# One-hot rows and weighted copies of the expert routing for eight tokens at once on VectorE, in 16-bit pairs

## The chip, the core and the metric

The kernel runs on one NeuronCore of a Trainium2 chip. Its engines are TensorE (PE in the profile, PEld for its weight loads), VectorE (DVE), ScalarE (ACT), GpSimd (POOL) and SyncE (SP, which issues most of the DMAs). Each engine works through its own queue in order and waits on semaphores for the others. The metric is the device time of one execution in microseconds; lower is better.

## What is computed

A 256-token model of two blocks, batch 1, width 1024, float32. The first block has three mixers side by side (state space, gated recurrence, retention) and a convolutional feed-forward network (FFN below). The second block has two layers over two streams of 256 tokens, latents and context; each layer mixes tokens (convolution, mLSTM, differential attention) and then applies PEER, a feed-forward layer of 16,384 small experts. The change concerns PEER:

```python
def peer_ffn(h, wq, sub_keys, eu, ev):
    def one(t):                                   # 128 tokens
        q = (t @ wq).reshape(128, 8, 2, 64)
        s = einsum("thpd,hpnd->thpn", q, sub_keys)
        st, it = top_k(s, 16)                     # of 128 keys, two halves
        cand = st[:, :, 0, :, None] + st[:, :, 1, None, :]
        cidx = it[:, :, 0, :, None] * 128 + it[:, :, 1, None, :]
        best, pos = top_k(cand, 16)
        e = take_along_axis(cidx, pos)            # 8 heads x 16 experts a token
        g = softmax(best)
        act = gelu(einsum("thkd,td->thk", eu[e], t))
        return einsum("thk,thkd->td", g * act, ev[e])
```

## The kernel before

PEER is computed densely. For every expert e = 128 n1 + n2 the products of all tokens with `eu` are formed, the gelu of them is multiplied by a dense matrix A[e, token] that holds the sum of the weights g of an expert chosen by that token and zero elsewhere, and the result goes through `ev`. Weights arrive as 512 KB pieces (`raw`); each is split into a high part on ACT (`whi`, L254) and a low part on DVE or POOL by turns (`wlo`, L255), and a product is 24 matmuls: high by high, high by low and low by high, over 8 k-tiles (L296, L297, L299).

A is made by `spread` (L1363 to L1400) from `sl`, which `choose` leaves for 128 tokens at a time: the two key numbers i1, i2 of each of the 128 slots (8 heads x 16), and g in two float16 parts. Slots lie on partitions. For each token a one-hot row over n1 and one over n2 is made by comparing an iota with i1 and i2; the row of n1 is multiplied by the two parts of g; two matmuls of 128x128 contract over the slots and add the token's A[n1, n2]. This goes in pieces of 4 tokens: two comparisons on DVE (`o2` L1375, `o1` L1380, 128x512, float32 in and float16 out), the weighted copies `ow` by shares on POOL (L1384), DVE (L1390) and ACT (L1392), 8 matmuls (L1395) into one of two PSUM banks, a copy into `stg` on ACT (L1396). Four pieces fill `stg` (1 MB), which SP writes to DRAM (L1399). 32 pieces make one call of `spread`; there are six calls.

In layer 0 `peer` runs both streams (512 columns a matmul). Its first 64 tiles of the first product (`first`, 24 matmuls and a gelu into `gt`, L1462) run "ahead", and the routing's pieces are recorded between them: half a tile for each piece of `choose`, then `early` (the context stream's two calls of `spread`, 100 pieces a tile for the first and 3 for the second), then the latents' two calls, 3 pieces a tile. In layer 1 (256 columns a matmul, 104 tiles ahead) 1.3 pieces of `spread` go with a tile. A scheduler then sets the order of each engine's queue from the dependences, a cost model and the recorded order, so the first call of `early` has filled gaps of the token mixing that stands before `peer`.

SBUF tiles lie in pools on a left and a right stack. A pool that takes the address range of an earlier one waits until that one is released. One such place matters below: the FFN of the first block (`ff8`: its normed input `fh`, `fl` and its hidden tiles) is on the left, while the context stream's token mixing of layer 0 runs on the right; the lowest of its pools is `m01d`, of the differential attention. In the program before, `ff8` ends at byte 128,608 of a partition and `m01d` begins at byte 128,704.

## Time and profile before

| | us |
|---|---|
| median of 3 runs (lowest to highest) | 4106.46 (4102.27 to 4113.05) |
| profiled execution, first to last instruction | 4098.2 |
| PE busy | 3722.7 (91%) |
| DVE busy | 2698.6 (66%) |
| ACT busy | 1785.9 (44%) |
| POOL busy | 1406.0 (34%) |

Shares of the whole span are averages over stages with different limits. The six calls of `spread` fall into three stretches: 986 to 1300 us (the first call of `early`, in gaps of the latents' token mixing), 1455 to 1770 us (the second call and the latents' two, in layer 0's ahead stage) and 3345 to 3592 us (layer 1). A stretch is read by four things: how busy each engine is in it, at what granted clock TensorE ran (1.00 is 2.4 GHz, 0.5 is 1.2 GHz, values between are mixtures), what TensorE waited for, and how many pieces and tiles were done.

### The profile page before, as it was taken

How to read it: one execution, taken by the hardware profiler on the slowest of the kernel's cores; microseconds unless marked ns; L12 is line 12 of the kernel's file. 1: busy time of each engine (PE TensorE's matmuls, PEld its weight loads, DVE VectorE, ACT ScalarE, POOL GpSimd, SP SyncE). 2: the span in 40 equal slices, each digit the busy share in tenths (PEclk: the TensorE clock that was granted, in tenths of full speed). 3: DMA queues.
4: the chain of work that ended last, by engine and by line, in shares of the span. 5: the costliest groups of instructions: out<-in, count | busy, mean ns of one | idle time of the engine just before them, and what ended most of it. 6: DMA issues, size and time to landing. Idle time of an engine off the chain costs nothing. (4 is left out here: it accounts for less than half of the span.)

```text
span 4098.2 us, 62119 instructions
## 1 busy us (share of the span) xinstructions
PE 3722.7 (91%) x23599; PEld 3237.8 (79%) x23599; DVE 2698.6 (66%) x5543; ACT 1785.9 (44%) x2944; POOL 1406.0 (34%) x904
## 2 busy tenths in 40 slices
PE   7899987987879988799999999999988887899998
PEld 6599987986857766677788888888876887789898
DVE  6745668689687788945553344443764899976765
ACT  3444456444565354432322233332462446644443
POOL 1132314255445675631111111111242557732222
PEclk9999998998989998999999999999999999999999
DMA  6654532443325444475663333433425546696764
GB/s 236 220 171 157 165 127 70 139 144 124 119 95 181 144 167 168 152 236 175 192 188 118 113 119 118 126 106 98 142 96 177 162 147 206 208 287 193 237 217 141
DMA packets 284122, 653.71 MB, mean 160 GB/s; under 512 B 21296, under 2 KB 139824, under 8 KB 277552
## 3 DMA queue, kind: packets, MB, share of 16 engines
q1 hardware_dynamic: 282960, 647.24, 48.7%
q8 instruction: 185, 3.03, 0.3%
q10 hardware_dynamic: 720, 1.47, 0.1%
q14 instruction: 113, 0.93, 0.1%
q0 software_dynamic: 144, 1.05, 0.1%
HBM read 574.70 MB, written 74.97 MB: 159 GB/s over the span
## 5 line engine op out<-in xcount | busy, mean ns | idle before, releaser
L255 POOL TENSOR_TENSOR wlo<-raw,whi 128x1024 fp32r<-128x1024 f32 x360 | 893.9, 2484 | 1994.4 <-ACT whi L254 836.5
L254 ACT ACTIVATE whi<-raw 128x1024 fp32r<-128x1024 f32 x836 | 882.4, 1057 | 1371.9 <-PE pp L1545 521.8
L255 DVE TENSOR_TENSOR wlo<-raw,whi 128x1024 fp32r<-128x1024 f32 x476 | 612.2, 1286 | 334.1 <-ACT whi L254 258.0
L296 PE MATMUL pp<-Hh,whi 128*128 128x256 f32 (+1 forms) x2176 | 717.5, 349 | 4.3 <-ACT whi L254 3.1
L297 PE MATMUL pp<-Hl,whi 128*128 128x256 f32 (+1 forms) x2176 | 705.9, 344 | 0.0
L1544 PE MATMUL pp<-yh,whi 128*128 128x512 f32 (+1 forms) x2048 | 650.6, 340 | 18.0 <-ACT yh L254 16.3
L1545 PE MATMUL pp<-yl,whi 128*128 128x512 f32 (+1 forms) x2048 | 654.1, 341 | 12.6 <-DVE yl L255 12.5
L296 PEld LDWEIGHTS pp<-Hh,whi 128*128 128x128 f32 x2176 | 427.1, 197 | 50.6 <-ACT whi L254 3.9
L297 PEld LDWEIGHTS pp<-Hl,whi 128*128 128x128 f32 x2176 | 427.3, 197 | 44.3 <-DVE ow L1390 0.9
L1544 PEld LDWEIGHTS pp<-yh,whi 128*128 128x128 f32 x2048 | 386.5, 190 | 67.8 <-ACT yh L254 23.7
L299 PE MATMUL pp<-Hh,wlo 128*128 128x256 f32 (+1 forms) x2176 | 420.0, 336 | 21.4 <-DVE wlo L255 19.4
L1545 PEld LDWEIGHTS pp<-yl,whi 128*128 128x128 f32 x2048 | 388.4, 191 | 62.1 <-DVE yl L255 19.2
L1549 DVE SCALAR_TENSOR_TENSOR xT<-pp,mod,xT 128x256 f32<-128x256 f32 x256 | 123.0, 481 | 443.0 <-PE pp L1547 442.6
L1547 PE MATMUL pp<-yh,wlo 128*128 128x512 f32 (+1 forms) x2048 | 398.2, 337 | 0.3 <-POOL wlo L255 0.3
L299 PEld LDWEIGHTS pp<-Hh,wlo 128*128 128x128 f32 x2176 | 343.0, 191 | 65.5 <-DVE wlo L255 21.0
L1547 PEld LDWEIGHTS pp<-yh,wlo 128*128 128x128 f32 x2048 | 323.9, 189 | 42.5 <-POOL wlo L255 0.5
L1531 DVE TENSOR_TENSOR gt<-gt,At 128x512 f32<-128x512 f32 (+1 forms) x256 | 206.2, 821 | 116.7 <-ACT gt L1462 70.2
L1395 PE MATMUL pm<-o,ow 128*128 128x128 f16 x1536 | 131.2, 229 | 121.9 <-DVE ow L1390 87.6
L1384 POOL TENSOR_TENSOR ow<-o,sl 128x512 f16<-128x512 f16 x128 | 187.8, 1472 | 135.2 <-DVE o L1380 115.7
L1395 PEld LDWEIGHTS <-ow 128*128 128x128 f16 x1536 | 97.6, 101 | 165.7 <-DVE ow L1390 124.0
L254 ACT ACTIVATE yh<-gt 128x512 fp32r<-128x512 f32 (+1 forms) x256 | 124.5, 518 | 225.3 <-DVE gt L1531 225.0
L1396 ACT ACTIVATE stg<-pm 128x512 f32<-128x512 f32 x192 | 192.7, 1056 | 61.7 <-PE pm L1395 41.4
(457 smaller groups left out, 6691.0 us busy)
## 6 DMA issues: line engine op xcount, KB each, us to landing
raw<-pu SPq DMA_DIRECT2D x256, 512.0 KB, 3.8
raw<-pv SPq DMA_DIRECT2D x256, 512.0 KB, 3.8
raw<-w SPq DMA_DIRECT2D x136, 512.0 KB, 3.6
aw<-ada SPq DMA_DIRECT2D x96, 512.0 KB, 4.4
A<-stg SPq DMA_DIRECT2D x48, 1024.0 KB, 5.7
At<-A SPq DMA_DIRECT2D x48, 1024.0 KB, 7.9
raw<-wf SPq DMA_DIRECT2D x72, 512.0 KB, 3.6
raw<-wo SPq DMA_DIRECT2D x32, 512.0 KB, 4.2
```

The costliest lines, as they stand in the source:

```text
L254: A.activation(hi, src, AF.Copy)
L255: (eng or V).tensor_sub(lo, src, hi.bitcast(F32))
L296: PE.matmul(ps, wh[:, k], xh[:, x0 + k], start=start and j == 0, stop=False)
L297: PE.matmul(ps, wh[:, k], xl[:, x0 + k], start=False, stop=False)
L299: PE.matmul(ps, wl[:, k], xh[:, x0 + k], start=False, stop=stop and j == len(ks) - 1)
L1384: G.tensor_mul(ow[:, na:], o1[:, na:, None].to_broadcast([P, nw, 2, P]), sl[:, 2:4, t0 + na:t0 + 4].rearrange("p j e -> p e j")[:, :, :, None]
L1395: PE.matmul(ps[:, e * P:(e + 1) * P], ow[:, e, j], o2[:, e], start=j == 0, stop=j == 1)
L1396: A.activation(stg[:, :, 4 * q4:4 * q4 + 4].rearrange("p n e -> p e n"), ps.rearrange("p (e n) -> p e n", e=4), AF.Copy, scale=1.0 / GSCALE)
L1531: V.tensor_mul(gt.rearrange("p (a t) -> p a t", t=16), gt.rearrange("p (a t) -> p a t", t=16), At[g][:, :, j])
L1544: PE.matmul(ps, wh[:, j], yh, start=j == 0, stop=False)
L1545: PE.matmul(ps, wh[:, j], yl, start=False, stop=False)
L1547: PE.matmul(ps, wl[:, j], Y[g, j][0], start=False, stop=j == 7)
```

## The change

`spread` handles 8 tokens (TB) at a time. The tile `sl` becomes float16 and holds every number twice: i1 beside i2, each as [token][n1 or n2], then g's high part beside its low part, with pairs that have the layout [2 kinds][token][pair]. An iota in float16, `iota16` (256 bytes a partition, in the permanent pool `perm`), is made once. One comparison on DVE gives the one-hot rows of both n1 and n2 of 8 tokens (`oo`, 128x2048, all operands float16, innermost dimension of two neighbouring elements) and one product on DVE gives both weighted copies (`ow`, 128x2048). POOL and ACT make none any more. The matmuls are the same in number and size; a piece is now every second token of a block, so that `stg` holds [n2 group][4 token pairs][8 n2][2 tokens] and the copy from PSUM writes elements 8 bytes apart where it wrote them 64 bytes apart. A keeps its size in DRAM; the multiplication in the main stage reads it in runs of 2 elements where it read runs of 16. `oo` and `ow` have two buffers each, in `early` `ow` has one. Layer 1 keeps 51 tiles in SBUF where it kept 52.

```diff
+    iota16 = perm.tile([P, P], F16, name="iota16")
+    V.tensor_copy(iota16, iota)
...
-        A.activation(sl[:, :2].rearrange("p j t -> p (j t)"), pt[:, :2 * P], AF.Copy)
-        hi = sm.tile([P, P], F16, name="ghi")
-        A.activation(hi, pt[:, 2 * P:3 * P], AF.Copy, scale=GSCALE)
-        V.tensor_copy(sl[:, 2], hi)
-        V.scalar_tensor_tensor(sl[:, 3], pt[:, 2 * P:3 * P], GSCALE, hi, op0=ALU.mult, op1=ALU.subtract)
+        twice = [P, P, 2]
+        for j in range(2):
+            A.activation(sl[:, 0, :, j], pt[:, j * P:(j + 1) * P][:, :, None].to_broadcast(twice), AF.Copy)
+        g = pt[:, 2 * P:3 * P][:, :, None].to_broadcast(twice)
+        A.activation(sl[:, 1, :, 0], g, AF.Copy, scale=GSCALE)
+        V.scalar_tensor_tensor(sl[:, 1, :, 1], g, GSCALE, sl[:, 1, :, 0], op0=ALU.mult, op1=ALU.subtract)
...
-    def spread(sl, Ad, t, sm, bank, share):
+    def spread(sl, Ad, t, sm, bank, ows=2):
+        wide = [P, TB, 2, P // 2, 2]
         for tg in range(8):
-            stg = sm.tile([P, P, 16], F32, name="stg")     # [n1][n2][16 t]
-            for q4 in range(4):
...
-                o2 = sm.tile([P, 4, P], F16, name="o2", bufs=O2)
-                if nd:
-                    V.tensor_tensor(o2[:, :nd], iota[:, None].to_broadcast([P, nd, P]),
-                                    sl[:, 1, t0:t0 + nd][:, :, None].to_broadcast([P, nd, P]), op=ALU.is_equal)
...
-                V.tensor_tensor(o1, iota[:, None].to_broadcast([P, 4, P]),
-                                sl[:, 0, t0:t0 + 4][:, :, None].to_broadcast([P, 4, P]), op=ALU.is_equal)
...
-                    G.tensor_mul(ow[:, na:], o1[:, na:, None].to_broadcast([P, nw, 2, P]),
...
-                            V.tensor_scalar(ow[:, e, j], o1[:, e], sl[:, 2 + j, t0 + e:t0 + e + 1], None, op0=ALU.mult)
...
-                        A.activation(ow[:, e, j], o1[:, e], AF.Copy, scale=sl[:, 2 + j, t0 + e:t0 + e + 1])
...
+            stg = sm.tile([P, 16, 8, 8, 2], F32, name="stg")
+            for b in range(16 // TB):
+                t0 = tg * 16 + b * TB
+                ix, gg = [sl[:, m, t0:t0 + TB][:, :, :, None].to_broadcast(wide) for m in range(2)]
+                oo = sm.tile([P, TB, 2, P], F16, name="oo", bufs=2)
+                V.tensor_tensor(oo.rearrange("p t j (n k) -> p t j n k", k=2),
+                                iota16.rearrange("p (n k) -> p n k", k=2)[:, None, None].to_broadcast(wide), ix,
+                                op=ALU.is_equal)
+                ow = sm.tile([P, TB, 2, P], F16, name="ow", bufs=ows)
+                V.tensor_tensor(ow.rearrange("p t j (n k) -> p t j n k", k=2),
+                                oo[:, :, 0].rearrange("p t (n k) -> p t n k", k=2)[:, :, None].to_broadcast(wide), gg,
+                                op=ALU.mult)
+                for k in range(2):
+                    ps = bank()
+                    for e in range(4):
+                        for j in range(2):
+                            PE.matmul(ps[:, e * P:(e + 1) * P], ow[:, 2 * e + k, j], oo[:, 2 * e + k, 1],
+                                      start=j == 0, stop=j == 1)
+                    A.activation(stg[:, :, 4 * b:4 * b + 4, :, k].rearrange("p g e n -> p e g n"),
+                                 ps.rearrange("p (e g n) -> p e g n", e=4, g=16), AF.Copy, scale=1.0 / GSCALE)
...
-            V.tensor_mul(gt.rearrange("p (a t) -> p a t", t=16), gt.rearrange("p (a t) -> p a t", t=16),
-                         At[g][:, :, j])
+            gv = gt.rearrange("p (a e k) -> p a e k", e=8, k=2)
+            V.tensor_mul(gv, gv, At[g][:, :, :, j])
...
-        peer(1, (0,), 13, 4, 52)
+        peer(1, (0,), 13, 4, 51)
```

The 256 bytes of `iota16` move every pool of the left stack up by as much. In the program after, `ff8` ends at byte 128,864, which is 160 bytes above the start of `m01d`.

DVE's queue in the latents' `spread` of layer 0 (`sl`; line 1375 is the comparison in both programs, 1380 the second one of before, 1390 the products of before, 1379 the product of after). Before:

```order
L1375 TENSOR_TENSOR o2_17427<-gen_65,sl_13240 128x512
L1380 TENSOR_TENSOR o1_17429<-gen_65,sl_13240 128x512
L1380 TENSOR_TENSOR o1_17483<-gen_65,sl_13240 128x512
L1390 TENSOR_SCALAR ow_17431<-o1_17429,sl_13240 128x128 x4
L1380 TENSOR_TENSOR o1_17505<-gen_65,sl_13241 128x512
L1375 TENSOR_TENSOR o2_17481<-gen_65,sl_13240 128x512
L1390 TENSOR_SCALAR ow_17485<-o1_17483,sl_13240 128x128 x4
```

And after:

```order
L1375 TENSOR_TENSOR oo_16504<-iota16_71,sl_13240 128x2048
L1379 TENSOR_TENSOR ow_16506<-oo_16504,sl_13240 128x2048
L1375 TENSOR_TENSOR oo_16530<-iota16_71,sl_13240 128x2048
L1379 TENSOR_TENSOR ow_16532<-oo_16530,sl_13240 128x2048
L1375 TENSOR_TENSOR oo_16588<-iota16_71,sl_13240 128x2048
```

Six instructions of DVE for every 4 tokens have become two for every 8, and nothing else stands between them.

DVE's queue where the first call of `early` (`ksl`) runs among the final norm of the first block (`rq`, `xT`). Before:

```order
L1380 TENSOR_TENSOR o1_14905<-gen_65,ksl_5211 128x512
L330 SCALAR_TENSOR_TENSOR rq_10731<-rq_10731 128x2
L1375 TENSOR_TENSOR o2_14923<-gen_65,ksl_5211 128x512
L1390 TENSOR_SCALAR ow_14907<-o1_14905,ksl_5211 128x128
L782 SCALAR_TENSOR_TENSOR xT_60<-xT_60,par_67,pm_10698 128x256 x8
L1390 TENSOR_SCALAR ow_14907<-o1_14905,ksl_5211 128x128
```

And after:

```order
L1375 TENSOR_TENSOR oo_14918<-iota16_71,ksl_5213 128x2048
L329 SCALAR_TENSOR_TENSOR rq_10731<-rq_10731 128x2
L1379 TENSOR_TENSOR ow_14894<-oo_14892,ksl_5213 128x2048
L330 TENSOR_TENSOR rq_10731<-rq_10731 128x2
L331 SCALAR_TENSOR_TENSOR rq_10731<-rq_10731 128x2
L783 SCALAR_TENSOR_TENSOR xT_60<-xT_60,par_67,pm_10698 128x256 x8
L1379 TENSOR_TENSOR ow_14920<-oo_14918,ksl_5213 128x2048
```

The same gaps are taken, by instructions four to sixteen times as wide; the second `ow` here has to wait until TensorE has read the first, because there is one buffer.

ACT's queue where the normed input `fh` of the FFN is first written (`kdk` is a projection of the context's token mixing, `pairh` the output of its attention). Before:

```order
L1007 ACTIVATE kdk_5208<-pp_5415 128x256
L254 ACTIVATE whi_5450<-raw_5448 128x1024
L361 ACTIVATE fh_7512<-t1_7562 128x256
L254 ACTIVATE whi_5482<-raw_5480 128x1024
L1007 ACTIVATE kdk_5208<-pp_5447 128x256
L361 ACTIVATE fh_7512<-t1_7566 128x256
```

And after:

```order
L255 ACTIVATE pairh_6189<-t1_6488 128x256
L255 ACTIVATE whi_6889<-raw_6887 128x1024
L1136 ACTIVATE t1_6639<-t1_6639 128x128
L1149 ACTIVATE t2_6644<-pp_6615 128x260
L255 ACTIVATE pairh_6189<-t1_6590 128x256
L362 ACTIVATE fh_7514<-t1_7564 128x256
```

`fh` has moved from the context's first projections to behind the last output of its attention, `pairh`, some 160 instructions further down ACT's queue. On TensorE's queue, with the other matmuls counted, 397 matmuls of the FFN stood ahead of the 4200th other one before, and 161 after. Of the second call of `early`, 2 pieces stood ahead of the choice of the latents' experts on TensorE's queue and 10 do now; from the latents' `spread` on, that queue is the same in both programs apart from names, but for a few matmuls near its end.

## Rows read from the trace of the kernel before

**Rows 1.** The page's first line.

```profile
span 4098.2 us, 62119 instructions
```

**Rows 2.** Busy time by stretch: PE, PEld, DVE, ACT, POOL; granted clock, DMA share, GB/s.

```profile
1455.00:1770.00 315.00, 255.27 (x1517) 200.86 (x1516) 293.20 (x477) 155.93 (x217) 195.48 (x123) 0.91 0.46 163
3345.00:3592.00 247.00, 199.98 (x1773) 191.59 (x1772) 238.48 (x333) 162.93 (x296) 171.78 (x95) 0.94 0.61 200
986.00:1300.00 314.00, 253.07 (x1713) 212.91 (x1712) 243.05 (x573) 183.16 (x393) 142.14 (x115) 0.87 0.37 124
...
520.00:674.00 154.00, 134.83 (x918) 120.72 (x918) 112.54 (x290) 99.45 (x219) 48.67 (x51) 0.97 0.28 93
674.00:1000.00 326.00, 276.30 (x2070) 265.10 (x2071) 265.43 (x737) 133.88 (x213) 140.06 (x97) 0.93 0.42 141
...
440.00:480.00 40.00, 40.00 (x340) 39.81 (x340) 29.96 (x35) 19.26 (x29) 10.37 (x5) 1.00 0.55 178
2000.00:2500.00 500.00, 498.87 (x2177) 408.06 (x2176) 219.00 (x293) 151.76 (x185) 72.59 (x30) 1.00 0.46 142
3600.00:3650.00 50.00, 46.42 (x361) 44.28 (x360) 40.80 (x75) 22.12 (x37) 14.66 (x6) 0.97 0.94 290
3700.00:4098.00 398.00, 370.69 (x3034) 364.85 (x3032) 245.15 (x370) 169.89 (x249) 101.43 (x41) 0.98 0.62 198
```

**Rows 3.** DVE's instructions on the one-hot rows alone, by stretch (busy, count).

```profile
986.00:1300.00 314.00, 77.07 (x146) 0.87 0.37 124
1455.00:1770.00 315.00, 290.67 (x474) 0.91 0.46 163
3345.00:3592.00 247.00, 189.46 (x239) 0.94 0.61 200
```

**Rows 4.** What PE waited for, 1455 to 1770 us: total, times, longest.

```profile
PE pm L1395 <- DVE ow L1390: 35.7, 28, 2.1
PE pm L1395 <- ACT stg L1396: 24.0, 30, 3.9
```

**Rows 5.** What PE waited for, 3345 to 3592 us.

```profile
PE pm L1395 <- DVE ow L1390: 40.3, 22, 2.9
```

**Rows 6.** ACT's copies into `stg` by stretch: one for each piece.

```profile
1455.00:1770.00 315.00, 91.40 (x95) 0.91 0.46 163
3345.00:3592.00 247.00, 65.72 (x62) 0.94 0.61 200
```

**Rows 7.** ACT's gelu into `gt` by stretch: one for each tile.

```profile
1455.00:1770.00 315.00, 19.12 (x32) 0.91 0.46 163
3345.00:3592.00 247.00, 19.33 (x53) 0.94 0.61 200
```

**Rows 8.** DVE by line: ns min/median/max, first and last start, forms.

```profile
L1375 DVE TENSOR_TENSOR o<-gen,sl x128: 673/680/2909, 1383.0 to 3592.1; 128x512 f16<-128x512 f32 x128
...
L1390 DVE TENSOR_SCALAR ow<-o,sl x384: 228/244/2451, 1387.7 to 3595.1; 128x128 f16<-128x128 f16 x192
...
L255 DVE TENSOR_TENSOR wlo<-raw,whi x476: 1154/1219/3433, 14.5 to 4076.1; 128x1024 fp32r<-128x1024 f32 x159
...
L373 DVE TENSOR_SCALAR t<-t x6: 172/276/841, 34.8 to 2912.1; 36x256 f32<-36x256 f32 x4, 16x256 f32<-16x256 f32 x1, 128x8 f32<-128x8 f32 x1
...
L380 DVE SCALAR_TENSOR_TENSOR t<-t,t x36: 158/406/949, 41.1 to 2924.2; 36x256 f32<-36x256 f32 x24, 16x256 f32<-16x256 f32 x6, 128x8 f32<-128x8 f32 x6
```

**Rows 9.** ACT by form: busy, mean ns of one, idle before and its releasers.

```profile
L1396 ACT ACTIVATE stg<-pm 128x512 f32<-128x512 f32 x192 | 192.7, 1056 | 61.7 <-PE pm L1395 41.4 <-issue 20.2
...
L1462 ACT ACTIVATE gt<-pp 128x512 f32<-128x512 f32 x128 | 76.5, 597 | 86.4 <-PE pp L299 84.2 <-DMA GX<-gt 1.4 <-DMA raw<-pu 0.7
```

**Rows 10.** POOL's splits `wlo` alone, 1455 to 1770 us.

```profile
1455.00:1770.00 315.00, 80.40 (x33) 0.91 0.46 163
```

**Rows 11.** PE's matmuls on `fh`, then on `fl`, 520 to 674 us.

```profile
520.00:674.00 154.00, 24.29 (x104) 0.97 0.28 93
...
520.00:674.00 154.00, 14.99 (x56) 0.97 0.28 93
```

More of the change, by code (lines that the diff above doesn't have):

```diff
@@ L25 @@
 GSCALE = 32768.0
-E0 = (0, 2, 1)
-O1, O2, OW = 2, 3, 3
+TB = 8
 def _cols(v):
@@ L1469, in peer @@
             q = queries(l, W, bk, sp, [z[:, :, j * T:(j + 1) * T] for z in (Hh, Hl)])
-            sls = [sp.tile([P, 4, P], F32, name="sl") for t in range(2)]
+            sls = [sp.tile([P, 2, P, 2, 2], F16, name="sl") for t in range(2)]
             bo = bo or Banks(ls, f"po{l}", 0, 2)
@@ L1485, in pieces @@
                     mark(f"spread{l}{s}")
-                    for _ in spread(sls[t], Ads[j], t, so, bo.misc, lambda n: (0, 2, ns)):
+                    for _ in spread(sls[t], Ads[j], t, so, bo.misc):
                         yield (1.3, 3.0)[1 - l]
@@ L1622, in build @@
                 a.wout()
-            early = [(100 if t == 0 else 3, spread(sls[t], A01, t, so, ax.misc, lambda n, t=t: E0)) for t in range(2)]
+            early = [(100 if t == 0 else 3, spread(sls[t], A01, t, so, ax.misc, 1)) for t in range(2)]
             def side(st):
```

34 lines of the change are left out of this document (7 added, 27 removed).

## The prediction

> **What bounds the kernel now.** I first read the page's span, 4098.2 us [rows 1], then the busy times by stretch, because the change touches only the stretches in which the expert matrix A is spread. In two of them DVE is the limit. From 1455 to 1770 us (layer 0, 512 columns) it is busy 293.2 of 315.0 us; from 3345 to 3592 us (layer 1, 256 columns) 238.5 of 247.0 us. PE is busy 81% in both, at a granted clock of 0.91 and 0.94 [rows 2]. What fills DVE there is the work that is replaced: 290.7 and 189.5 us on one-hot rows and their copies [rows 3]. PE waits for those copies: 35.7 us in the first stretch, with another 24.0 us for ACT's copy of a PSUM bank [rows 4], and 40.3 us in the second [rows 5]. The reader should also see that DVE's busy time holds waiting: a copy takes 0.244 us in the median and 2.451 us at worst, a comparison 0.680 and 2.909 [rows 8]. The longest are as long as one of POOL's splits, 80.4 us for 33 or 2.44 us each [rows 10]. In layer 0's stretch the 95 pieces hold 190 comparisons and 31 x 2 + 64 x 4 = 318 copies, 207 us by their medians; the other 84 of the 290.7 are hindrance, under 195 us of POOL's work. In the first spreading stretch, 986 to 1300 us, nobody is the limit: DVE 243 of 314 us, PE 253 [rows 2], and spreading is 77 us of it [rows 3].
>
> **What TensorE needs if nothing holds it up.** A 512-column matmul costs 498.87/2177 = 0.229 us at full clock, a 256-column one 40.00/340 = 0.118 us [rows 2]; for one of 128 columns I take a quarter of the first, 0.057 us. Layer 0's stretch has 95 pieces [rows 6] and 32 tiles [rows 7]: 32 x 24 x 0.229 + 95 x 8 x 0.057 = 176 + 43 = 219 us, against 315 that it takes. Layer 1's has 62 pieces and 53 tiles: 53 x 24 x 0.118 + 62 x 8 x 0.057 = 150 + 28 = 178 us, against 247. (The 8 pieces that the second call of `early` now puts ahead of the choice are 4 us of PE in either place.)
>
> **The new DVE instructions.** Two of 2048 columns for 8 tokens, so one for each piece of 4. No 16-bit instruction with two tensor inputs stands in the trace. Upper bound: two float32 inputs cost 0.680 us at 512 columns and 1.219 at 1024 [rows 8], 0.539 more for 512, so 2.30 us at 2048. Lower bound: as for half the columns, 1.22 us. I take the lower one. The trace shows that this engine does two columns a step where a form allows it: 256 columns take 0.276 us in a one-input instruction and 0.406 in a two-input one, in the same float32 [rows 8]; the new operands are laid out as pairs of 16 bits. The Trainium skill, page VectorE: DVE Perf Modes, section The perf-mode tier table, gives a 16-bit two-input instruction of 2048 columns 1224 ns and a float32 one 2293; by it the sum stands as I make it, and no run here shows it yet. Collisions with POOL add to either: 84 us under 195 us of POOL's work make about 34 under the 80 that stay, for 95 instructions some 0.3 us each.
>
> *Layer 0's stretch.* DVE: 95 x 1.22 = 116 us, 144 with collisions, far below 219, so PE sets the pace. To its 219 us come the waits for a PSUM bank: two banks stay, and these were 24.0 us. ACT's copy takes 1.056 us where a contiguous one of the same size takes 0.597 [rows 9]; the new writes are 8 bytes apart and not 64, the cost lies between these two, and I take half of the wait, 12 us. In the 16 blocks of `early` `ow` has one buffer: the next product waits for TensorE, which waits for it, 1.22 us at most where no tile stands between, some 11 times, 13 us; I take 8. Sum 239, a gain of 76. Bounds: 95 with neither wait, 36 with both whole and the clock left at 0.91 (219/0.91 + 37 = 278). ACT loses its share of the copies and POOL 116 us of work; neither was the limit, so that is worth nothing by itself.
>
> *Layer 1's stretch.* DVE: 62 x 1.22 = 76 us and the 49 us that are not spreading (238.5 less 189.5), 125 in all; with collisions 144. PE's 178 us is the floor, but the transfers come near: 200 GB/s over 247 us would have to pass in 178 us, 278 GB/s, and the densest stretch shows 290 at a DMA share of 0.94 [rows 2]. I take 195 us, a gain of 52; bounds 69 (PE alone) and 25 (DVE unpacked with collisions, 62 x 2.58 + 49 = 209, and 13 of other waits).
>
> *The first call of early.* Its 32 pieces leave DVE 39 us of work where 77 stood. DVE is one of several engines waited for there, so I take a quarter of the 38, a gain of 10. Bounds: all 38, and a loss of 20: with one buffer of `ow`, DVE can stand in front of each of 16 products for 1.22 us, and the norms and attention queued behind it on DVE, then PE and ACT, wait too.
>
> *iota16.* Its cast is one short instruction. Its 256 bytes are not free: `ff8` now reaches 160 bytes into `m01d`, so `fh` is not written before the context's attention is over. Before, TensorE did 104 + 56 = 160 of the FFN's matmuls by 674 us [rows 11], 160 x 0.118 = 19 us; by the queues the lag grows to 397 - 161 = 236 matmuls, 28 us. All of it costs if PE was idle there otherwise, nothing if the context's mixing ends earlier by as much. PE was busy 135 of 154 us until 674 and then 276 of 326 with DVE at 265 [rows 2], so both in part: a loss of 12, bounds 0 and 28.
>
> *Main stages.* The multiplication by A reads runs of 8 bytes. If that cost 0.23 us more for 256 columns (half of 1.056 less 0.597), layer 1's 128 would be 29 us of DVE, in a stretch where it is idle 153 of 398 us [rows 2]: 0, at most a loss of 10. In layer 0 PE is busy 498.87 of 500 us and hides it. The one tile more through DRAM is 128 KB each way, under 1 us.
>
> Sum: +12 - 10 - 76 - 52 + 0 = -126 us. On the profiled execution's 4098.2 us that is 3972; the median of the runs, 4106.46, lies 8.3 us higher, and 3980 is my time.
>
> **The rivals.** *Unpacked*: the instructions take 2.30 us. DVE then needs 95 x 2.58 = 245 us in layer 0 and 209 in layer 1, 6 and 14 more than the sum has, and the first call gains nothing (10): 3980 + 30 = 4010. Against it: the two-columns row; for it: that row is of another form.
>
> *Unpacked and in turn with POOL*: DVE and POOL wait for each other's whole instruction, so their times add. Layer 0: 95 x 2.30 + 80 = 299 us, 60 more than the sum; layer 1: 62 x 2.30 + 49 + 27 splits x 2.44 = 258, no gain but a start 11 us later, taken as 247 to 258 and 57 more; the first call 10: about 4107, no change. Packed, adding gives 116 + 80 = 196 us, and nothing changes. Against it: today 207 us of unhindered DVE work and 195 of POOL's fit into 315 us, so 87 us at least ran together; for it, the 2.45 us stalls. The Trainium skill, page SBUF — State Buffer, section SBUF: two separate sides, says that a DVE instruction with two SBUF inputs and a GpSimd one that reads SBUF take a shared port pair in turn, for the whole instruction; the stalls agree with it, the 87 us do not.
>
> *Side effects*: the FFN's lag costs its 28 and the first call its loss of 20: 3980 + 16 + 30 = 4026. For it: DVE and PE are both dense from 674 to 1000 us. Against it: PE is busy 88% of the time before 674 us, so the context's mixing has time to win there.
>
> *Slower*: pairs are read at a penalty, as ACT pays for scattered elements. The price from the same row is 0.46 us for 512 columns, so 2.30 + 4 x 0.46 = 4.14 us. Layer 0: 95 x 4.14 = 393, 78 more than now; layer 1: 62 x 4.14 + 49 = 306, 59 more; the first call 32 x 4.14 - 77 = 55, half of it; the FFN 12: 4106 + 176 = 4280. It decides from a mean of 3.3 us an instruction on (315/95), and 3.2 in layer 1. Nothing in the trace speaks for it but that ACT row.
>
> **How the numbers follow.** Forecast 0.72 (3900 to 4035), unpacked 0.11, in turn with POOL 0.04, side effects 0.09, slower 0.04. The bounds of the terms add up to -202 and about 0 us; all at one end is unlikely. The range 3900 to 4060 leaves out the slower case, the one in turn with POOL, and the tails of the others, under 2 in 10. Faster by over 0.3% (what a measurement of this kernel can tell from no change): 0.72 + 0.11 + 0.09 less a little, 0.91. Within 0.3%: 0.05. Slower: 0.04.
>
> **What would show it.** Right: the instructions of 2048 columns at 1.2 to 1.5 us; a tile and its three pieces in layer 0 every 7.5 us, where it was 9.8; PE's waits for DVE under 15 us in both stretches; DVE below 60% there; a clock near 1.00; `fh` first written near 685 us instead of 530. Wrong: instructions above 2 us; PE waiting for ACT or for transfers as long as it did for DVE; the context's mixing or the first call longer than before; a main stage that grows.

## The result, and the profile after

The changed kernel takes 3958.53 us (median of 4 runs, 3951.11 to 3968.15), the kernel before 4104.36 us beside it: a ratio of 0.9646 [0.9626, 0.9665], or 146 us less. The prediction was 3980, with a range of 3900 to 4060. The profiled execution of after has a span of 3966.4 us, 131.8 less than that of before [rows 1]; it is the longest of the four (3968.15 us), and the kernel's repetition below has a span of 3951.4.

The two stretches of spreading, busy times by stretch (columns: length; PE, PEld, DVE, ACT, POOL busy; granted clock; DMA share; GB/s). First layer 0 with 512 columns, then layer 1 with 256:

```profile
core 0: us, PE busy (x) PEld busy (x) DVE busy (x) ACT busy (x) POOL busy (x), PEclk, DMA share, GB/s
1478.00:1690.00 212.00, 202.62 (x1363) 162.99 (x1361) 139.47 (x79) 93.49 (x143) 69.33 (x30) 1.00 0.62 215
3285.00:3453.00 168.00, 166.88 (x1649) 164.71 (x1648) 136.60 (x86) 103.49 (x165) 66.72 (x24) 1.00 0.84 283
```

Where DVE was busy 93 and 97% and PE 81% [rows 2], PE is now busy 96 and 99% at full clock. What PE still waits for in the first of them (us in total, times, longest), where [rows 4] had 35.7 and 24.0:

```profile
PE pm L1387 <- DVE ow L1379: 7.8, 5, 1.8
PE pm L1387 <- ACT stg L1389: 1.4, 1, 1.4
```

In the second there is only one wait of 1.1 us, for `stg`, where [rows 5] had 40.3 us for `ow`.

The new instructions, by tile (shortest/median/longest in ns); `ksl` is the context's call, `sl` the latents' and layer 1's:

```profile
L1375 DVE TENSOR_TENSOR oo<-iota,ksl x32: 1180/1218/3422, 1001.1 to 1530.9; 128x2048 f16<-128x2048 f16 x32
L1375 DVE TENSOR_TENSOR oo<-iota,sl x64: 1208/2652/3470, 1385.2 to 3442.2; 128x2048 f16<-128x2048 f16 x64
L1379 DVE TENSOR_TENSOR ow<-oo,sl x64: 1200/1225/3360, 1389.2 to 3443.5; 128x2048 f16<-128x2048 f16 x64
```

Undisturbed they take the 1.22 us that was predicted. But half of the comparisons of `sl` take 2.65 us or more. That cost TensorE little here, but the experiments turn on it.

To see where the time went, the span is cut at five places that every kernel has, each read as the start of a group of instructions: the end of the FFN (first `xT` of the final norm), layer 0's normed input (first `Hh`), the start of its main stage (first product of `gt` with `At`), layer 1's normed input (last `Hh`), and the last copy into `stg`. Lengths in us, of one profiled execution each:

| kernel | to the FFN's end | token mixing with the first call of `early` | layer 0 ahead | layer 0 main, layer 1's mixing | layer 1 ahead, to the last `stg` | rest |
|---|---|---|---|---|---|---|
| before | 1011.1 | 246.9 | 552.1 | 1347.3 | 438.6 | 502.2 |
| after | 1025.7 | 237.4 | 465.8 | 1348.9 | 374.9 | 513.7 |
| after, again | 1018.3 | 240.0 | 465.3 | 1346.2 | 371.7 | 509.9 |
| iota kept in the old one | 1007.4 | 236.9 | 464.8 | 1348.6 | 373.7 | 508.6 |
| old `stg` layout | 1016.0 | 237.7 | 475.7 | 1348.8 | 372.9 | 505.9 |
| unpacked | 1024.7 | 280.4 | 518.1 | 1345.9 | 433.0 | 505.2 |
| GpSimd products, in heaps | 1014.8 | 236.7 | 508.7 | 1346.8 | 428.5 | 508.2 |
| GpSimd products, spaced | 1019.4 | 238.7 | 491.3 | 1347.7 | 412.2 | 504.3 |
| half of A not written | 1015.9 | 242.3 | 466.5 | 1349.7 | 373.9 | 517.9 |
| four tokens in `early` | 1013.9 | 240.2 | 479.6 | 1351.7 | 376.1 | 512.0 |
| VectorE's splits ahead | 1009.4 | 242.1 | 465.6 | 1347.4 | 359.8 | 512.6 |
| two of three GpSimd's | 1009.9 | 237.3 | 463.5 | 1350.0 | 379.9 | 511.6 |
| VectorE's splits in all of layer 1 | 1004.8 | 242.3 | 463.8 | 1348.4 | 360.2 | 473.9 |

The gain of 131.8 us is -86.3 in layer 0's ahead stage, -63.7 in layer 1's, -9.5 in the first call of `early`, and +14.6, +1.6 and +11.5 in the rest (rounded).

### The profile page after: what moved, and what is told of

The parts are those of the page before. It is cut to its first block, busy times and chain, and to the rows that moved or that the text cites. A ratio compares the mean times of both kernels' runs of the same rounds, so it can differ in the third digit from the quotient of the medians.

```text
span 3966.4 us, 60653 instructions
## 1 busy us (share of the span) xinstructions
PE 3678.3 (93%) x23599; PEld 3209.1 (81%) x23599; DVE 2418.7 (61%) x4834; ACT 1647.4 (42%) x2692; POOL 1137.7 (29%) x712
## 5 line engine op out<-in xcount | busy, mean ns | idle before, releaser
L297 PE MATMUL pp<-Hh,whi 128*128 128x256 f32 (+1 forms) x2176 | 695.5, 340 | 2.4 <-ACT Hh L365 1.2
L298 PE MATMUL pp<-Hl,whi 128*128 128x256 f32 (+1 forms) x2176 | 683.0, 334 | 0.0
L297 PEld LDWEIGHTS pp<-Hh,whi 128*128 128x128 f32 x2176 | 411.1, 189 | 43.3 <-ACT whi L255 1.6
L298 PEld LDWEIGHTS pp<-Hl,whi 128*128 128x128 f32 x2176 | 411.2, 189 | 42.3 <-DVE Hl L366 0.9
L256 DVE TENSOR_TENSOR yl<-gt,yh 128x512 fp32r<-128x512 f32 (+1 forms) x256 | 149.9, 612 | 93.9 <-ACT yh L255 93.1
L297 PE MATMUL pp<-pairh,whi 128*128 128x256 f32 x672 | 174.6, 294 | 13.7 <-ACT t L1055 5.4
L1375 DVE TENSOR_TENSOR oo<-iota,sl 128x2048 f16<-128x2048 f16 x64 | 136.3, 2130 | 62.1 <-PE pm L1387 56.3
L298 PE MATMUL pp<-pairl,whi 128*128 128x256 f32 x672 | 172.4, 291 | 1.8 <-DVE pairl L256 1.7
## 6 DMA issues: line engine op xcount, KB each, us to landing
raw<-pu SPq DMA_DIRECT2D x256, 512.0 KB, 3.9
raw<-pv SPq DMA_DIRECT2D x256, 512.0 KB, 3.9
raw<-w SPq DMA_DIRECT2D x136, 512.0 KB, 3.5
aw<-ada SPq DMA_DIRECT2D x96, 512.0 KB, 4.5
raw<-wf SPq DMA_DIRECT2D x72, 512.0 KB, 3.5
raw<-wo SPq DMA_DIRECT2D x32, 512.0 KB, 3.7
```

Of the source, the lines that this page charges most:

```text
L256: (eng or V).tensor_sub(lo, src, hi.bitcast(F32))
L297: PE.matmul(ps, wh[:, k], xh[:, x0 + k], start=start and j == 0, stop=False)
L298: PE.matmul(ps, wh[:, k], xl[:, x0 + k], start=False, stop=False)
L1375: V.tensor_tensor(oo.rearrange("p t j (n k) -> p t j n k", k=2), iota16.rearrange("p (n k) -> p n k", k=2)[:, None, None].to_broadcast(wid ...
```

## Experiments

Medians are of 4 to 11 runs. The variants ran in four groups, and in each the kernel before ran on the same chip: the repetition, the moved iota, the old layout and the interleaved spreading on one chip; the unpacked form, GpSimd's products in heaps, half of A and four tokens on that chip again; the spaced products and the first two runs on the splits on a second; the last run on a third. Where a run is compared with one of another group, the difference by the ratios to the kernel before is given beside that of the medians.

**The changed kernel again.**

> The changed kernel again, beside three variants on one chip, so that differences of a few us between them can be read. Every theory: 3958 us within 8, ratio to the kernel before 0.963 to 0.967. What is to be seen beside the time: layer 0's stretch of spreading at TensorE's floor again (PE busy over 200 of 212 us, clock 1.00), and the main stage of layer 1 about 513 us after the last copy from PSUM, where the kernel before had 502; if that returns to 502 the 11 us are scatter and not a consequence.

3953.18 us, ratio 0.9639 [0.9627, 0.9652]. The stretches repeat within 3 us. The last column does not return to 502, but it scatters over several us between kernels that are alike there.

**The overlap of pools.** The float16 iota is put into the upper half of the float32 one, of which only 16 columns are read elsewhere; so no pool moves.

```diff
-    iota16 = perm.tile([P, P], F16, name="iota16")
-    V.tensor_copy(iota16, iota)
+    with TP("i16") as tmp:
+        t16 = tmp.tile([P, P], F16, name="t16")
+        V.tensor_copy(t16, iota)
+        iota16 = gen[:, 3 * P + 64:4 * P].bitcast(F16)
+        V.tensor_copy(iota16, t16)
```

> The float16 iota is kept in the unused upper half of the float32 iota and takes no bytes of its own; no pool moves and the FFN's input no longer overlaps the differential attention's pool. Theory: that overlap costs what was read from the two traces, 8 us at the end of the FFN: fh first written near 530 us again instead of 678, the FFN's end 8 us earlier, time 8 us (4 to 14) below the changed kernel. Rival A: it costs the whole lag that the queues show, 28 us, and the time falls by 20 or more. Rival B: it costs nothing, since the context's token mixing gets longer by what the FFN's early start takes from it (17 us longer in the kernel before than in the changed one): time within 3 us of the changed kernel.

3941.66 us, 11.5 below the repetition; ratio 0.9612 [0.9599, 0.9626]. By tile and line, the first and last start of the FFN's input and of the final norm, in after:

```profile
L362 ACT ACTIVATE fh<-t x8: 399/416/419, 678.2 to 684.0; 128x256 fp32r<-128x256 f32 x8
L783 DVE SCALAR_TENSOR_TENSOR xT<-xT,par,pm x8: 476/476/481, 1025.7 to 1028.5; 128x256 f32<-128x256 f32 x8
```

and in this variant:

```profile
L365 ACT ACTIVATE fh<-t x8: 399/408/419, 528.0 to 549.0; 128x256 fp32r<-128x256 f32 x8
L786 DVE SCALAR_TENSOR_TENSOR xT<-xT,par,pm x8: 472/472/479, 1007.4 to 1010.1; 128x256 f32<-128x256 f32 x8
```

`fh` is written 150 us earlier, and 18 us of that are left at the FFN's end (11 against the repetition, 3 of which are there already at the end of the first mixers). The 11 arrive whole at the end of the kernel. Both rivals, 20 us or more and nothing, fall.

**The old layout of `stg` and A.**

```diff
-            stg = sm.tile([P, 16, 8, 8, 2], F32, name="stg")
+            stg = sm.tile([P, P, 16], F32, name="stg")
...
-                    A.activation(stg[:, :, 4 * b:4 * b + 4, :, k].rearrange("p g e n -> p e g n"),
-                                 ps.rearrange("p (e g n) -> p e g n", e=4, g=16), AF.Copy, scale=1.0 / GSCALE)
+                    A.activation(stg[:, :, TB * b + k:TB * b + TB:2].rearrange("p n e -> p e n"),
+                                 ps.rearrange("p (e n) -> p e n", e=4), AF.Copy, scale=1.0 / GSCALE)
```

> The two new instructions stay; the copy from PSUM goes back to elements 64 bytes apart and A to its old layout. Theory of the prediction: the copy takes 1.056 us again instead of 0.627, and with two PSUM banks TensorE waits for it as before: 12 to 24 us more in layer 0, some 6 to 15 in layer 1, time 12 to 35 us above the changed kernel. Rival: the 24 us of before were the bunching of pieces behind VectorE's copies, and with an even flow two banks are enough: TensorE waits under 5 us for the copy, time within 5 us of the changed kernel.

3960.8 us, 7.6 above the repetition; ratio 0.9664 [0.965, 0.9678]. The line of the copy, and who waited for it:

```profile
L1389 ACT ACTIVATE stg<-pm x192: 1015/1086/1185, 1006.8 to 3451.1; 128x512 f32<-128x512 f32 x192
  PE pm L1387: 20.5, 32
```

The same rows of the repetition are 592/627/662 ns and 2.3 us. So the waits come back (20.5 us in all; [rows 4] had 24.0 in one stretch), but their price is between the two theories: 10 us in layer 0 and 1 in layer 1.

**Layer 1's spreading among the choice.** On top of the variant with the iota moved, the first 32 pieces of spreading are recorded between those of the second choice:

```diff
+                    sg = spread(sls[0], Ads[j], 0, so, bo.misc)
+                    for _ in choose(l, q, 1, sls[1], sm, bks.proj, bk):
+                        yield 2.0
...
+                        next(sg, None)
+                        yield 2.0
...
```

> As the variant with the iota kept in the old one's upper half, and in layer 1 the spreading of the first 128 tokens is recorded between the pieces of the second choice, so that A's writes to DRAM begin earlier. Theory: the 11 us that layer 1's main stage gave back come from transfers (DMA share 0.84 in the stretch of spreading and 0.94 just behind it, weights late), and TensorE is idle 25 of 205 us in the choice, where spreading can fill in: DMA share below 0.75 in the whole ahead stage, 5 to 25 us less than that variant. Rival: the choice is a chain of VectorE instructions (58 of 65 us busy) and gets longer by each 1.2 us instruction put into it: no change, or up to 15 us more.

3958.86 us, 17 above that variant. The last `stg` comes 39 us earlier, but ahead and main stage together take 897 us and not 882. PE now waits 19.2 us for `ow` in the choice, where DVE is busy 57 of 60 us. That is a little more than the rival's 15 us, and the theory falls.

**Unpacked.** The changed kernel with one repeated element in place of pairs:

```diff
-                ix, gg = [sl[:, m, t0:t0 + TB][:, :, :, None].to_broadcast(wide) for m in range(2)]
+                ix, gg = [sl[:, m, t0:t0 + TB, :, 0:1].to_broadcast([P, TB, 2, P]) for m in range(2)]
```

> The changed kernel with one thing undone: the comparison and the product read the token's number as one element repeated 128 times (innermost step 0) and not as pairs; sizes, types, counts and order of everything else stay. Theory of the prediction: the instructions take about 2.3 us instead of 1.2, VectorE is busy some 200 us longer in all (192 instructions), but TensorE keeps the pace for most of it: 15 to 40 us more than the changed kernel (its 3953 to 3958 us), most of it as waits for ow in the two stretches. Rival A: VectorE's time is itself what was gained, and 200 us more of it cost 80 us or more. Rival B: the form with step 0 runs at the same 1.2 us, and nothing changes.

4111.03 us, ratio 1.0021 [1.0012, 1.003]: the whole gain is gone. The instructions are as expected:

```profile
L1375 DVE TENSOR_TENSOR oo<-iota,sl x64: 2271/2283/4504, 1433.3 to 3591.5; 128x2048 f16<-128x2048 f16 x64
L1377 DVE TENSOR_TENSOR ow<-oo,sl x64: 2266/2292/4499, 1438.4 to 3595.7; 128x2048 f16<-128x2048 f16 x64
```

But the two stretches, by busy time, are DVE's again:

```profile
1525.00:1790.00 265.00, 219.37 (x1376) 172.91 (x1375) 223.07 (x77) 96.07 (x144) 95.22 (x31) 0.96 0.50 175
3385.00:3602.00 217.00, 180.43 (x1626) 174.94 (x1625) 210.47 (x85) 101.94 (x159) 71.82 (x24) 0.92 0.65 215
```

77 instructions of 2.28 us are 176, and the row shows 223 us. Rival A is nearest, and the theory of the prediction falls. By the table, 53 us went in layer 0's ahead stage, 61 in layer 1's and 40 in the first call of `early`.

What fills those 223 us can be seen one instruction at a time in any kernel with the new spreading. The timeline of the repetition, where the instructions are packed (start, us, engine), DVE's and POOL's rows alone, around two splits:

```profile
1602.94 2.39 POOL L256 TENSOR_TENSOR wlo<-raw,whi 128x1024 fp32r<-128x1024 f32 x1 [4.76 <-PE pp L300]
1603.74 2.66 DVE L1375 TENSOR_TENSOR oo<-iota,sl 128x2048 f16<-128x2048 f16 x1 [0.84 <-PE pm L1387]
1606.44 1.23 DVE L1379 TENSOR_TENSOR ow<-oo,sl 128x2048 f16<-128x2048 f16 x1
...
1610.10 2.39 POOL L256 TENSOR_TENSOR wlo<-raw,whi 128x1024 fp32r<-128x1024 f32 x1 [4.78 <-PE pp L300]
1610.46 3.10 DVE L1375 TENSOR_TENSOR oo<-iota,sl 128x2048 f16<-128x2048 f16 x1 [2.79 <-PE pm L1387]
```

The first split ends at 1605.33, the comparison at 1606.40, 1.07 us later; the second at 1612.49 and 1613.56, 1.07 later again. It is not only these two: in this execution 46 of VectorE's instructions of 2048 columns begin during a split, and 45 of them end 1.07 to 1.08 us behind its end, however early they began. The 126 that meet no instruction of POOL take 1.19 to 1.23 us. In the unpacked execution 47 of 49 end 2.14 to 2.15 us behind the split that they began in. The other way round it is the same:

```profile
3347.21 1.23 DVE L1379 TENSOR_TENSOR ow<-oo,sl 128x2048 f16<-128x2048 f16 x1
3347.31 3.39 POOL L256 TENSOR_TENSOR wlo<-raw,whi 128x1024 fp32r<-128x1024 f32 x1 [4.74 <-ACT whi L255]
```

The 17 splits that begin during such an instruction end 2.2 to 2.3 us behind its end, so they last up to 3.4 us, where an undisturbed one takes 2.34. So the new theory was: the two engines take turns, by whole instructions.

**GpSimd's products put back.** In the latents' calls and in layer 1 GpSimd makes a product for each piece as before, which nobody uses; for its room layer 1 keeps 50 tiles and not 51.

```diff
+                    if ows == 1:
+                        pass
+                    else:
+                        pd = sm.tile([P, 2, 2, P], F16, name="pd", bufs=1)
+                        G.tensor_mul(pd, iota16[:, None, None].to_broadcast([P, 2, 2, P]),
+                                     sl[:, 1, t0 + 2 * k:t0 + 2 * k + 2, :, 0:1].to_broadcast([P, 2, 2, P]))
```

> The changed kernel, and for each piece of the latents' calls and of layer 1's GpSimd makes a product of 128x512 float16 as it did before (its result is used by nobody, so this is work added and the output is the same); one tile more of layer 1 passes through DRAM to make room. 128 instructions of 1.37 us are 175 us more of GpSimd. Theory of the prediction: GpSimd's relief was worth nothing by itself: within 5 us of the changed kernel, though VectorE's instructions are held up longer. Rival: the two engines hinder each other, so that part of the gain is GpSimd's silence: VectorE's mean instruction grows from 1.5 to 2 us or more, TensorE waits, and 15 to 40 us come back.

4050.22 us, ratio 0.987 [0.9855, 0.9886], 97 us back. As an experiment it was badly made: the products depend on `sl` alone, so they ran as soon as they could. POOL's products by stretch (busy us, count):

```profile
1480.00:1520.00 40.00, 28.51 (x24) 0.73 0.29 88
1520.00:1735.00 215.00, 0.00 (x0) 0.99 0.63 219
```

In front of the splits, in heaps, they made TensorE wait for weights: it was busy 18 of those 40 us. So it was made again, each product reading the rows of its own block:

```diff
-                        G.tensor_mul(pd, iota16[:, None, None].to_broadcast([P, 2, 2, P]),
+                        G.tensor_mul(pd, oo[:, 2 * k:2 * k + 2, 0:1].to_broadcast([P, 2, 2, P]),
```

> As the run with GpSimd's added products, but each product reads the one-hot rows of its own block (oo), so that it can't run ahead of its piece and lie in a heap before the spreading; 64 instructions of 1.04 us in each layer lie between the pieces, as in the kernel before. Theory: VectorE's instructions with two inputs in SBUF and GpSimd's take turns, whole instruction by whole instruction. In layer 0 that is 96 us of VectorE, 72 of GpSimd's splits and 67 of products, 235 us against a stretch of 217: 15 to 40 us more there. In layer 1 it is 106 of VectorE, 58 and 67 of GpSimd, 231 us against 166: 40 to 65 us more. In all 55 to 105 us above the changed kernel (3953 to 3958 us). Rival: they run side by side, the heap alone cost the 97 us of the first form, and VectorE (106 us) and GpSimd (125) both fit below TensorE's floor: within 10 us of the changed kernel.

4018.6 us, ratio 0.9795 [0.9777, 0.9813], 65 us above the repetition (64 by the ratios): 26 in layer 0's ahead stage, 40 in layer 1's. Side by side, it would have been under 10. Layer 1's stretch by busy time, then its groups of POOL and DVE (count, busy us, mean ns):

```profile
3330.00:3509.00 179.00, 153.16 (x1420) 148.20 (x1420) 162.21 (x74) 84.17 (x141) 172.76 (x76) 0.96 0.69 235
```

```profile
L1379 DVE TENSOR_TENSOR ow<-oo,sl 128x2048 f16<-128x2048 f16 x27 | 57.7, 2137 | 0.9
L1375 DVE TENSOR_TENSOR oo<-iota,sl 128x2048 f16<-128x2048 f16 x26 | 54.8, 2109 | 0.0
L256 DVE TENSOR_TENSOR wlo<-raw,whi 128x1024 fp32r<-128x1024 f32 x21 | 53.4, 2543 | 10.7 <-ACT whi L255 10.3
L1388 POOL TENSOR_TENSOR pd<-oo,sl 128x512 f16<-128x512 f16 x54 | 102.5, 1898 | 3.8 <-DVE oo L1375 1.2
L256 POOL TENSOR_TENSOR wlo<-raw,whi 128x1024 fp32r<-128x1024 f32 x22 | 72.6, 3301 | 1.6 <-ACT whi L255 1.6
```

The two engines show 91 and 97% busy, but much of that is waiting: undisturbed, DVE's 53 instructions of 1.22 and 21 splits of 1.29 us are 92 us, POOL's 54 products of 1.03 and 22 splits of 2.34 are 107. Together 199 us stand in 179, in turn but for a tenth. Some four tenths of each engine's busy time are waiting for the other (162 us against 92, 173 against 107).

**Half of A not written.**

```diff
-                    if (b, k) == (16 // TB - 1, 1):
+                    if (b, k) == (16 // TB - 1, 1) and not (half and tg % 2):
```

> The changed kernel with every second write of A in layer 1 left out (8.4 of 16.8 MB; the other half of A is read from layer 0's matrix of the context, so the number of bytes read stays and the output is another). Theory: the 4 to 11 us that layer 1's main stage lasts longer than in the kernel before (502 there, 505 to 513 in four kernels with the new spreading) come from transfers still queued when it begins: with 29 us of transfers fewer it lasts 502 or less and the time is 5 to 10 us below the changed kernel; the stretch of spreading, at TensorE's floor, does not get shorter. Rival: the difference is the clock and scatter: main stage 505 to 513 again, time within 3 us.

3964.1 us, ratio 0.9655 [0.964, 0.9669]; the rest after the last `stg` takes 517.9 us, the longest of all. The writes of A are not its cause, and the theory falls. The bytes read stayed as they were, so reads are not tested by this run.

**Four tokens in `early`.** Two pairs of instructions of 1024 columns in place of one of 2048, with two buffers each, in the context's calls alone. `choose` stores the tokens of a block in the order of the pieces, in all six calls, and needs 6 instructions on ACT for 3 and 4 on DVE for 1 to write them.

```diff
+                for k in (0, 1) if ows == 1 else (0,):
+                    n = TB // 2 if ows == 1 else TB
...
+                    ow = sm.tile([P, n, 2, P], F16, name="ow", bufs=2)
```

> As the variant with the iota kept in the old one's upper half (3942 us); in the context's two calls the two instructions are made for 4 tokens and not for 8, twice as many at half the size, so that ow has two buffers in less room than the one took; tokens lie in sl in another order for it. Theory of the prediction: the single buffer costs TensorE's waits for ow, 7.8 us in the second call, and something of the same kind in the first: 5 to 10 us less than that variant. Rival A: the waits move to the next engine in turn and nothing is gained, within 3 us. Rival B: the second set of fixed costs (64 instructions more on VectorE) eats it: 3 to 8 us more.

3966.24 us, ratio 0.9658 [0.9644, 0.9671], 25 above the variant that it is built on (19 by the ratios), so rival B and worse. Layer 0's ahead stage is 15 us longer, and PE's waits for `ow` in it grew from 8.9 to 18.3 us. That two small buffers cover less time than the one large one did would explain it, but was not tried by itself, and neither were the added instructions of `choose`. The first call gained nothing.

**Who makes the splits.** If the engines take turns, a split on GpSimd (2.4 us) takes more from VectorE than one that VectorE makes itself (1.2 us). Built on the variant with the iota moved:

```diff
-            W.pattern = "G" if ns > 1 else "GV"
+            W.pattern = "G" if ns > 1 else "V"
```

> As the variant with the iota in the old one's upper half (3942 us), and in layer 1's ahead stage every split of a weight's low part is VectorE's, none GpSimd's. Theory (in turn): without GpSimd's splits the comparison in layer 1's spreading falls from a mean of 1.93 us to 1.25 or less, although VectorE gets 24 splits of 1.29 us more there; the stretch stays at TensorE's floor. In the choice VectorE's splits fall from 2.03 to 1.3 us, 48 of them instead of 24: 62 us instead of 49, so up to 13 us more there. Time 0 to 12 us above that variant. Rival (side by side): 24 splits more in the choice, where VectorE is busy 53 of 60 us, cost their whole 31 us, and the comparison stays near 1.9 us.

and with "GGV" in the same place:

> The opposite of the run with VectorE alone: of three splits in layer 1's ahead stage two are GpSimd's. TensorE waits 21 us in the choice for splits of VectorE. Theory (in turn): each split moved takes 2.4 us in which VectorE's two-input instructions stand still, for 1.3 us that it is spared: nothing gained, within 5 us of the variant with the iota moved (3942 us), or more; the mean of the comparison in the spreading rises above 1.93 us. Rival (side by side): a third of VectorE's splits fewer, 8 to 15 us less.

VectorE alone: 3934.53 us, ratio 0.9585 [0.9569, 0.9602], 7 below (11 by the ratios). Two of three on GpSimd: 3953.98 us, ratio 0.9636 [0.9619, 0.9654], 12 above (10 by the ratios). The intervals of both overlap a little with that of the variant, 0.9612 [0.9599, 0.9626]; between the two, on one chip, lie 19 us, and the time rises with GpSimd's share. DVE's groups in layer 1's ahead stage (count, busy us, mean ns), of the variant that both are built on:

```profile
L259 DVE TENSOR_TENSOR wlo<-raw,whi 128x1024 fp32r<-128x1024 f32 x50 | 84.7, 1695 | 41.5 <-ACT whi L258 41.5
L1378 DVE TENSOR_TENSOR oo<-gen,sl 128x2048 f16<-128x2048 f16 x32 | 63.9, 1998 | 16.4 <-PE pm L1390 12.0 <-ACT sl L1362 4.4
```

of VectorE alone:

```profile
L259 DVE TENSOR_TENSOR wlo<-raw,whi 128x1024 fp32r<-128x1024 f32 x102 | 125.0, 1228 | 57.6 <-ACT whi L258 57.6
L1378 DVE TENSOR_TENSOR oo<-gen,sl 128x2048 f16<-128x2048 f16 x32 | 39.0, 1217 | 0.0
L1296 DVE CAST itf<-iu 128x64 f32<-128x64 uint32 x8 | 1.4, 174 | 0.0
L1326 DVE MAX8 st<-s 128x8 f32<-128x128 f32 x32 | 7.7, 280 | 0.7 <-ACT s L1323 0.7
```

and of two in three on GpSimd:

```profile
L1378 DVE TENSOR_TENSOR oo<-gen,sl 128x2048 f16<-128x2048 f16 x32 | 75.6, 2363 | 16.5 <-PE pm L1390 14.5 <-ACT sl L1362 2.0
L1296 DVE CAST itf<-iu 128x64 f32<-128x64 uint32 x8 | 17.5, 2192 | 0.0
L1326 DVE MAX8 st<-s 128x8 f32<-128x128 f32 x32 | 7.6, 278 | 4.9 <-ACT s L1323 4.9
```

With 52 splits more (5 at the stage's start are still GpSimd's) VectorE is busy 291 us of this stage, where it was 299: what it does more it no longer waits. The comparison's mean follows GpSimd's share, 1.22, 2.00, 2.36 us. The stage became 14 us shorter, better than the 0 to 12 us longer that I had expected; with GpSimd's share raised it became 6 us longer. In both, the theory in turn is right about the comparison and the rival is not.

**VectorE's splits in all of layer 1.** The last run carries the same into layer 1's main stage:

```diff
-        W.pattern = "VVG"
+        W.pattern = "VVG" if ns > 1 else "V"
```

> As the run in which VectorE makes all splits of layer 1's ahead stage (3934.5 us), and all those of layer 1's main stage too, where GpSimd made every third (42 of them, 2.48 us each). TensorE waits there 20 us for yh and 10 for yl, and behind both stands VectorE's product with A, 0.74 us in the mean where the shortest takes 0.41. Theory (in turn): the product's mean falls below 0.5 us, VectorE's 42 splits more (54 us) are partly paid by that, and with VectorE idle 190 of 513 us there the time is 2 to 12 us below that run. Rival (side by side): the product stays at 0.74, VectorE's queue grows by 54 us in front of yh and yl, and the time is 5 to 20 us above.

3896.19 us, ratio 0.9508 [0.9492, 0.9524], 38 below the last (32 by the ratios) and the best of all. After the last `stg`, DVE's groups of the run before:

```profile
L259 DVE TENSOR_TENSOR wlo<-raw,whi 128x1024 fp32r<-128x1024 f32 x104 | 131.9, 1268 | 40.6 <-ACT whi L258 40.2
L1528 DVE TENSOR_TENSOR gt<-gt,At 128x256 f32<-128x256 f32 x128 | 79.1, 640 | 36.0 <-DMA gt<-GX 19.9 <-DMA At<-A 9.1 <-ACT gt L1458 6.8
```

and of this one:

```profile
L259 DVE TENSOR_TENSOR wlo<-raw,whi 128x1024 fp32r<-128x1024 f32 x153 | 186.3, 1219 | 43.9 <-ACT whi L258 43.8
L1528 DVE TENSOR_TENSOR gt<-gt,At 128x256 f32<-128x256 f32 x128 | 50.5, 418 | 11.4 <-DMA gt<-GX 8.3 <-DMA At<-A 3.1
```

49 splits more, 54 us, and DVE is busy 332 us instead of 323. The product with A falls from 640 to 418 ns, and PE's waits for `yh` and `yl` behind it from 30 to 12 us. The direction was expected, the size (2 to 12 us) was not. Where the 38.7 us of this stage come from shows on TensorE (columns as above), in the run before and in this one:

```profile
3424.30:3936.90 512.60, 471.47 (x3804) 462.63 (x3803) 322.75 (x508) 216.31 (x320) 128.18 (x51) 0.97 0.67 209
3419.50:3893.40 473.90, 452.44 (x3804) 446.23 (x3803) 332.14 (x559) 216.25 (x320) 0.00 (x0) 0.99 0.71 226
```

Its waits for `yh` and `yl` are 18.5 us shorter, and the same 3804 matmuls are busy 19.0 us less, at a mean granted clock of 0.99 where it was 0.97. I had priced the waits alone. Fewer waits and a higher clock come together in these two rows; what raised the clock was not tried by itself.

## Why the prediction was right, and where it was not

**What bounded the kernel: half right.** VectorE set the pace of both stretches, and with its work cut TensorE does, at a clock of 1.00: a tile and its pieces take 212/29 = 7.3 us in layer 0 (7.5 was named). VectorE's busy share fell to 66 and 81%, not below 60, because its busy time, before and after, holds its own work and the waiting for GpSimd's.

**The new instructions: right.** 1.22 us undisturbed. The unpacked run shows the alternative, 2.28, as estimated (2.30). The Trainium skill, page VectorE: DVE Perf Modes, section Mode 2×_1P — pack two bf16 into one 32-bit read, asks for 16-bit elements at a step of one; the pair has it and the repeated element has not. The two measured durations, 1.22 and 2.28 us, agree with it.

**Layer 0: 76 predicted, 86 measured.** The floor held: by the prediction's prices the 29 tiles and 86 pieces of the stretch need 199 us, and PE is busy 203 of its 212. Of the two waits, that for `ow` was 8 and is 7.8; that for the copy was taken as half of 24 and is 1.4. Mis-sized was this second term: the copy takes 0.627 us, inside the bounds of 0.597 and 1.056 but almost at the lower one, and TensorE hardly waits for it. The run with the old layout shows what I had halved: 20.5 us of waits, 10 us of time.

**Layer 1: 52 predicted, 64 measured.** The step that failed was the allowance of 17 us for transfers. At 283 GB/s and a DMA share of 0.84 TensorE waits for none: the 49 tiles and 64 pieces of the stretch need 139 + 29 = 168 us by the prediction's prices, and the stretch takes 168. PE alone would have given the bound of 69.

**First call of `early`: 10 predicted, 9.5 measured.** The size came out, but the quarter that I took is not explained. Unpacked, its comparisons and products cost 35 us more of VectorE's time (75 for 40), and the stage gets 40 us longer, though they are then no more of it than the 77 us in the kernel before. That the longer instructions stand in other work's way would fit; halving them gained nothing there. This stays open.

**iota16: 12 predicted, 8.3 measured** (14.6 at the FFN's end less 6.3 by which this execution lagged already at the end of the first mixers), and 8 us by the variant without the overlap (11 at the FFN's end against the repetition, less 3 at the end of the first mixers). `fh` came at 678 us; 685 was named.

**Main stages: nothing taken, at most a loss of 10; 1.6 and 11.5 measured.** Layer 0's is TensorE's. Layer 1's lies outside the bound, and a main stage that grows was named as a sign of being wrong. Every kernel of the table with the new spreading and the old splits has 504 to 518 us after the last `stg`, the kernel before 502 in its one profile. I had looked for the cause at the product with A on VectorE, and it is not there: that takes 0.64 us in the mean and took 0.66, and VectorE is busy 321 us of this stage and was 320. TensorE shows the difference, before and then after:

```profile
3596.00:4098.20 502.20, 468.15 (x3804) 459.52 (x3803) 320.30 (x507) 216.37 (x320) 129.28 (x52) 0.98 0.67 214
3452.70:3966.40 513.70, 474.93 (x3804) 466.64 (x3803) 321.08 (x507) 216.22 (x320) 128.42 (x52) 0.96 0.67 210
```

The same matmuls are busy 6.8 us longer at a lower clock, and the waits for `yh` and `yl` are 27.9 us and were 22.5. In three other kernels with the new spreading (old `stg` layout, unpacked, spaced products) the clock is 0.97 or 0.98, the same matmuls are busy 468 to 469 us, and the stage takes 504 to 506. So the stage's length goes with the clock and these waits, as in the last run; what sets them in each execution stays open. Half of A's writes had no part in it.

**The rivals.** *Unpacked* was priced at 4010 us and is 4111. The one that I gave 0.04, *unpacked and in turn with POOL*, was priced at 4107, and its terms for the two layers hold: 60 us in layer 0 (53 measured) and 57 in layer 1 (61). That its total comes within 4 us of 4111 is partly luck: the first call of `early` costs 40 and not 10, and the sum starts from 3953 and not 3980. The step that failed is the argument against it, that 87 us "at least ran together". I had added medians of records. Records of one engine overlap, and records of both contain the wait for the other. In the timeline of the kernel before, at places where DVE did not wait for POOL:

```profile
1608.92 1.28 DVE L1380 TENSOR_TENSOR o<-gen,sl 128x512 f16<-128x512 f32 x2
1617.99 0.73 DVE L1390 TENSOR_SCALAR ow<-o,sl 128x128 f16<-128x128 f16 x4
```

Four copies take 0.73 us, not 4 x 0.244; two comparisons 1.28, not 1.36. From 1455 to 1770 us the 474 instructions that [rows 3] counts (I had worked out 508 from the pieces) are 300 copies, 55 us, and 174 comparisons, 111; POOL's 89 products at their shortest of 1.04 and 33 splits of 2.34 make 170. Together 336 us in 315: in turn to within 7%. From 3345 to 3592 us the same count (120 copies, 119 comparisons and 28 splits on VectorE, 61 products and 28 splits on POOL) makes 261 us in 247. So the two stretches of the kernel before were filled by the sum of two engines, and the sentence that GpSimd's 116 us less were "worth nothing by itself" was wrong: put back in four of the six calls, its products cost 65 of the 148 us. The forecast survived because, packed, the sum (116 + 80 us) stays under TensorE's floor, which the text said.

The Trainium skill, page SBUF — State Buffer, section SBUF: two separate sides, states the rule: GpSimd and an operation of VectorE in a mode with two ports hold a shared port pair in turn, for a whole instruction, and so does an operation of VectorE with two inputs in SBUF against one of GpSimd that reads SBUF. The runs agree with it: a comparison that begins during a split ends 1.07 to 1.08 us behind it, and its mean follows GpSimd's share. I had cited the rule and let the 87 us stand against it.

**The total.** That the sum of -126 us came within 6 of the profiled executions' -131.8 is in part luck. The two stretches gave 22 us more and the overlap cost 4 less; the main stages, taken at nothing, and the first mixers, which have no term, took 13 and 6 back. In the repetition the 6 are not there.

## What to carry to other kernels

Where VectorE and GpSimd work at the same time on SBUF, add their undisturbed times (shortest records, or those of back-to-back instructions without the other engine) and compare the sum with the stretch; the busy share of either says little, since it contains the wait for the other. Work given to GpSimd to relieve VectorE can cost more than it relieves: taking GpSimd's 2.4 us splits in layer 1 back to VectorE at 1.2 us left VectorE no busier (623 us of the two stages, 622 before) and made the kernel 45 us faster (43 by the ratios). A number that is to be spread over a row can be stored twice, side by side, in 16 bits (1.22 us for 2048 columns against 2.28); here the whole gain hung on it, since with the repeated element the kernel is back at 4111 us.

## What the runs showed of the hardware that I had not expected

- Not every form waits for GpSimd. With its share of splits the cast of 128x64 from uint32 goes from 174 to 2192 ns and the comparison from 1.22 to 2.36 us, but MAX8 stays at 278 to 280 ns. In the repetition the 94 MAX8 of 128 columns that lie within a split take 0.276 us in the median, the 98 others 0.273.
- GpSimd waits as much: with VectorE dense, its product takes 1.90 us in the mean for 1.03 undisturbed, its split 3.30 for 2.34.
- ScalarE's copy of a bank costs 0.627 us with elements 8 bytes apart and 1.086 with 64; the contiguous write of the same size, of another function (the gelu), takes 0.597 [rows 9].
